# Values, merge gates and branch outputs with tokens as rows, 512 weight channels per matmul

## The chip, the core and the metric

One core of one Trainium2 chip runs the kernel. The metric is the device time of one execution in microseconds (us). In the profile's names PE is TensorE's matmul and PEld its weight load, DVE is VectorE, ACT is ScalarE, POOL is GpSimd and SP issues the DMAs.

## What is computed

Two layers over 256 tokens of 1024 channels, float32. Each layer normalises its input, makes three branches from one wide projection, gates and merges them, projects and adds the residual:

```python
h = rms_norm(x, norm_w)
rq, rk, rv, rg, aq, ak, av, ag, cu, cg, mg = split(h @ w_in + b_in)
r = head_norm(retention(rope(rq), rope(rk), rv)) * ret_norm_w   # 4 heads of 256
y_ret = (r * silu(rg)) @ ret_w_o
a = three dilated attention groups, 8 heads of 128 each, merged by softmax over their sums
y_att = (a * silu(ag)) @ att_w_o
c = silu(layer_norm(causal depthwise conv, 31 taps, of c_lin * sigmoid(c_gate)))
y_conv = (c * silu(cg)) @ conv_w_o
g = sigmoid(mg)                                                  # three gates per channel
x = x + (g[0] * y_ret + g[1] * y_att + g[2] * y_conv) @ w_out
```

After the second layer a last rms_norm gives the output.

## The kernel before, in words

Every weight product is cut into units of 256 channels by 1024 inputs (1 MB), 96 for a layer; `order()` (L60) lists them as (layer, kind, i), and the loop at L802 runs them in that order. The kinds: `cs`, `cl` (convolution gate and input), `rq`, `rk`, `rv`, `rg` (retention), `aq`, `ak`, `av`, `ag` (attention), `cg` (convolution's gate), `mr`, `ma`, `mc` (merge gates), `yr`, `ya`, `yc` (branch outputs), `wo` (output projection).

A unit n goes through four steps. `load` (L171) brings its weights into one of three `raw` tiles, issued three units ahead. `split` (L181), written two units ahead, makes a high part `whi` on ACT (L194, two halves of 1024 columns) and a low part `wlo` on DVE (L195); both have five half-unit buffers, so the second half of unit n + 2 takes the buffer of the first half of unit n. `gemm` (L198) issues 48 products of 128x128 by 256 columns in fp32r: 8 chunks k of the contraction, two halves j, and three products (high x high, high x low, low x high) each. It has three PSUM banks (`g`) in rotation. `finish` (L684) reads the bank.

Most units put channels on the partitions and stream the 256 tokens; only `rv` and `av` put tokens there and stream 256 weight channels. The gates `merge_gate` (L601) are two ACT sigmoids of 256 columns with the bias as a column. `branch` (L607) multiplies product and gate on DVE, adds to `m`, and for `yc` writes `mh` (high on ACT, low on DVE through `hi_lo`, L232), which is the moving operand of `wo`.

Each engine runs what it was given in the order written. In one turn of the loop that is: load(n + 3), split(n + 2), the products of unit n (with the list `inside` in their middle), the list `first`, finish(n), the list `due`, and taps of the convolution, DVE pairs that are handed out by a credit of RATE - COST[kind] per unit, 0.79 for each. Other work is put at a unit by `later` (L717 to 763): scores, softmax and value products of attention, the sums of the convolution's layer norm (`ln_add` at ya 1, `ln_mean` at ya 2, `ln_rows` at ya 3 and mc 2, `ln_rstd` at mc 1).

Of the kernel before, what the change touches and what calls it, by code (L numbers as in the profile page):

```python
# [44 lines left out]
RATE = 2.85  # L45
# [10 lines left out]
COST = {"cs": 0.3, "cl": 1.1, "rq": 1.9, "rk": 1.9, "rv": 2.0, "rg": 1.2, "mr": 0.0, "yr": 0.6,  # L56
        "aq": 2.2, "ak": 2.2, "av": 0.8, "ma": 0.0, "ag": 1.2, "ya": 1.2, "mc": 0.0, "cg": 1.2, "yc": 1.8, "wo": 1.4}


def order():  # L60
    """(layer, kind, i) of every 256-column piece of the weights, in the order of use"""
    u = []
    for l in range(DEPTH):
        def put(kinds, ids):
            u.extend((l, kind, i) for i in ids for kind in kinds)

        def pair(p):
            put(("aq", "ak"), (p, 4 + p, 8 + p))
            put(("av",), (p, 4 + p, 8 + p))
# [11 lines left out]
        put(("ma",), (0,))  # L81
        put(("ag",), four)
        put(("ma",), (1, 2, 3))
        for kind in ("ya", "mc", "cg", "yc", "wo"):
            put((kind,), four)
    return u

# [43 lines left out]
def trunk(ctx: ExitStack, tc, xp, wp, b_in, params, consts, out):  # L131
# [24 lines left out]
    N = len(units)  # L156
    st = {}
# [10 lines left out]
    # ------------------------------------------------------------ weights  # L168
    raw_t, hi_t, lo_t = {}, {}, {}

    def load(n, parts=((0, NK),)):  # L171
        if n >= N:
            return
        t = sb.tile([128, NK, W], F32, tag="raw", name="raw", bufs=3)
        src = wp[n].rearrange("p (k n) -> p k n", n=W)
# [3 lines left out]
        raw_t[n] = t  # L179
# [18 lines left out]
    def gemm(n, a, tokens_first, k_first):  # L198
        """tokens_first: [tokens, channels] out of the product, else [channels, tokens]"""
        hs, ls = hi_t.pop(n), lo_t.pop(n)  # L200
        if n + 1 < N:
# [5 lines left out]
        def part(j, k):  # L207
            wh, wl = hs[k // 4][:, k % 4, :], ls[k // 4][:, k % 4, :]
            t = slice(j * 128, j * 128 + 128)
            if tokens_first:  # L210
                trio = ((a[:, k, 0, t], wh), (a[:, k, 0, t], wl), (a[:, k, 1, t], wh))
            else:
                trio = ((wh[:, t], a[:, k, 0, :]), (wh[:, t], a[:, k, 1, :]), (wl[:, t], a[:, k, 0, :]))
# [17 lines left out]

    def hi_lo(dst, k, v, nk, n=None):  # L232
        """dst: [128, 8, 2, S]; v: fp32 [128, nk, S]"""
# [9 lines left out]
    # ------------------------------------------------------------ norms  # L243
# [3 lines left out]
    def token_sums(tiles, ss=None, more=False):  # L247
        """sums over the partitions of the [128, S] tiles, [tokens, 2]"""
# [35 lines left out]
    def add_squares(key, v, start, stop):  # L284
        """st[key] (+)= v ** 2, two tiles, one of them at the stop"""
# [9 lines left out]
    def unscaled(l, k):  # L295
        """tile k of x * norm_w, before the rstd"""
# [31 lines left out]
    # ------------------------------------------------------------ convolution  # L328
# [77 lines left out]
    # ------------------------------------------------------------ rope  # L406
# [27 lines left out]
    def bias_rows(l, key, c0):  # L434
        bb = sb.tile([128, W], F32, tag="bb", name="bb")
        SP.dma_start(bb, b_in[l:l + 1, c0:c0 + W].to_broadcast([128, W]))
        st[key, "bb"] = bb

    def values(key, p):
        v = sb.tile([128, 2, W], F32, tag="v", name="v")  # L440
        DVE.tensor_tensor(v, p, two(st.pop((key, "bb"))), ALU.add)
        st[key] = v

    def stacked_values(l, pair, g, bb, p):
        """[:, r, c] holds the keys t % 4 == 2 * r + c of both dilated groups: the first of them
        on partitions 64 * c.., the second on the other half."""
        if g == 1:
            st[l, "vs", pair] = sb.tile([128, 2, 2, W], F32, tag="vs", name="vs", bufs=1)
        vs = st[l, "vs", pair]
# [18 lines left out]
    def ret_out(l, h):  # L468
# [9 lines left out]
        rn = sb.tile([128, 2, W], F32, tag="rn", name="rn", bufs=1)  # L478
# [101 lines left out]
    # ------------------------------------------------------------ gates and merge  # L580
# [20 lines left out]
    def merge_gate(l, i, b, p):  # L601
        g = sb.tile([128, 2, S], F32, tag="gt", name="mg", bufs=4)
        for j in range(2):
            ACT.activation(g[:, j], p[:, j], AF.Sigmoid, bias=col(l, P_B + MG // 128 + 8 * b + 2 * i + j))
        st[l, "mg", i] = g

    def branch(l, i, b, n, p):  # L607
        g = st.pop((l, "mg", i))
        if b == 0:
            if i == 0:  # L610
                st[l, "m"] = sb.tile([128, NK, S], F32, tag="m", name="m", bufs=1)
            DVE.tensor_tensor(st[l, "m"][:, 2 * i:2 * i + 2], p, g, ALU.mult)
            return
        m = st[l, "m"][:, 2 * i:2 * i + 2]
        DVE.tensor_tensor(g, p, g, ALU.mult)
        DVE.tensor_tensor(m, m, g, ALU.add)
        if b == 2:
            if i == 0:
                st[l, "mh"] = sb.tile([128, NK, 2, S], F32R, tag="h", name="mh", bufs=1)
            hi_lo(st[l, "mh"], 2 * i, m, 2, n if i < 3 else None)  # L620
# [15 lines left out]
    # ------------------------------------------------------------ end  # L636
# [46 lines left out]
    # ------------------------------------------------------------ program  # L683
    def finish(n, p):  # L684
        l, kind, i = units[n]
# [8 lines left out]
        elif kind in ("rv", "av"):  # L694
            if kind == "av" and i >= 4:
                stacked_values(l, i % 4, i // 4, st.pop((units[n], "bb")), p)
            else:
                values(units[n], p)
        elif kind in ("rg", "ag", "cg"):
            gated(l, i, COLS[kind][1], "c" if kind == "cg" else "ru", n, p)  # L700
        elif kind in ("mr", "ma", "mc"):
            merge_gate(l, i, "rac".index(kind[1]), p)
        elif kind in ("yr", "ya", "yc"):
            branch(l, i, ("r", "a", "c").index(kind[1]), n, p)
        elif l + 1 < DEPTH:
            project(l, i, n, p)
        else:
            project_last(l, i, n, p if n + 1 == N else halves(p))
# [8 lines left out]
    for l in range(DEPTH):  # L717
        for i in range(4):
            b = pos[l, "rq", i]
            later(b + 3, ret_scores, l, i)  # L720
            later(b + 5, ret_out, l, i, at=first)
            later(b + 7, ret_back, l, i, at=first)
# [42 lines left out]
    def warm_up():  # L765
        """keeps the tensor engine busy until the first operands are there, for its clock"""
# [10 lines left out]
    with tc.manual_schedule():  # L777
# [24 lines left out]
        for n, (l, kind, i) in enumerate(units):  # L802
# [6 lines left out]
            if kind in ("rv", "av"):  # L809
# [73 lines left out]
```

## Time and profile before

| | us |
|---|---|
| median of 3 runs | 1215.42 |
| lowest, highest | 1214.85, 1216.55 |
| span of the profiled execution | 1212.8 |
| PE busy | 1202.6 (99% of the span) |
| DVE busy | 994.5 (82%) |
| ACT busy | 742.4 (61%) |
| 16 DMA engines, share of their time | 49% |

The span runs from the first to the last instruction on the core and is 2.6 us under the median of the timed runs; the profiled execution has no time of its own beside it. PE's busy time comes from modelled ends of pipelined matmuls, so how fast it goes is read from the distance of starts and from the length of stretches with a known count, not from the length of one matmul.

### The profile page before, as it was taken

To read this page: it belongs to the slowest core of one execution; us is meant where nothing else is said; L and a number is where in the kernel's file an instruction comes from. 1 tells how busy PE (TensorE), PEld (TensorE's weight loads), DVE (VectorE), ACT (ScalarE), POOL (GpSimd) and SP (SyncE) were. 2 spreads that over 40 slices of the span, in tenths; PEclk is the share of its full clock that TensorE was granted. 3 is DMA by queue.
4 is the path that set the end of the run, shared out by engine and by line. 5 is a ranking of instruction groups with operands and counts; after the bars stand their busy time and mean duration, and the time that the engine had idled before them with its cause. 6 is when DMAs were issued, how large, how long until landed. Compare 5 with 4: busy or idle time off the path is not lost.

```text
span 1212.8 us, 24142 instructions
## 1 busy us (share of the span) xinstructions
PE 1202.6 (99%) x9924; PEld 1195.9 (99%) x9924; DVE 994.5 (82%) x1825; ACT 742.4 (61%) x1140; POOL 9.2 (1%) x17
## 2 busy tenths in 40 slices
PE   9999999999999999999999999999999999999997
PEld 8999999999999999999999999999999999999997
DVE  6988798888888899667789887988898988868674
ACT  6644566759495857366555445587676766664652
POOL 0000000000000000000000000000000000000000
PEclk9999999999999999999999999999999999999999
DMA  8644355445454545555445444544454545455540
GB/s 329 239 161 168 139 202 181 178 148 179 148 179 148 181 160 195 189 181 188 174 161 199 176 148 154 200 178 169 152 178 175 174 154 178 149 209 174 178 170 36
DMA packets 35101, 211.53 MB, mean 174 GB/s; under 512 B 3888, under 2 KB 8752, under 8 KB 10544
## 3 DMA queue, kind: packets, MB, share of 16 engines
q1 hardware_dynamic: 34992, 210.00, 48.8%
q8 instruction: 78, 1.28, 0.4%
q14 instruction: 31, 0.25, 0.1%
HBM read 208.94 MB, written 1.05 MB: 173 GB/s over the span
## 4 chain that ended last, share of the span: by engine, by line
PE 89%; issue 7%; DVE 2%; ACT 1%; DMA 0%; SPq 0%; POOLq 0%; POOL 0%; DVEq 0%; ACTq 0%
PE g L215 82%; PE as L518 2%; PE u L577 1%; PE pt L560 1%; DVE wlo L195 1%; PE rs L459 1%; PE u L573 1%; DMA raw<-in_wp 0%; PE rs L461 0%; PE u L574 0%; PE rt L491 0%; PE r L472 0%; PE r L473 0%; PE r L471 0%; DVE cacc L361 0%
## 5 line engine op out<-in xcount | busy, mean ns | idle before, releaser
L195 DVE TENSOR_TENSOR wlo<-raw,whi 128x1024 fp32r<-128x1024 f32 (+1 forms) x387 | 454.9, 1213 | 76.6 <-ACT whi L194 75.1
L194 ACT CAST whi<-raw 128x1024 fp32r<-128x1024 f32 (+1 forms) x387 | 390.5, 1040 | 135.0 <-PE g L215 127.2
L215 PE MATMUL g<-h,whi 128*128 128x256 f32 x2432 | 439.4, 283 | 0.0
L215 PEld LDWEIGHTS g<-h,whi 128*128 128x128 f32 x2432 | 374.6, 189 | 0.4
L215 PE MATMUL g<-h,wlo 128*128 128x256 f32 x1216 | 343.1, 282 | 0.0
L215 PE MATMUL g<-hp,whi 128*128 128x256 f32 x1280 | 234.0, 285 | 0.0
L215 PEld LDWEIGHTS g<-h,wlo 128*128 128x128 f32 x1216 | 229.3, 189 | 0.0
L361 DVE SCALAR_TENSOR_TENSOR cacc<-cpad,prm,cacc 128x256 f32<-128x256 f32 x480 | 200.9, 480 | 2.2 <-ACT cacc L358 1.9
L215 PEld LDWEIGHTS g<-hp,whi 128*128 128x128 f32 x1280 | 199.9, 192 | 0.4
L215 PE MATMUL g<-hp,wlo 128*128 128x256 f32 x640 | 181.2, 283 | 0.2 <-DVE wlo L195 0.2
L215 PE MATMUL g<-gated,whi 128*128 128x256 f32 x768 | 138.7, 283 | 0.0
L215 PEld LDWEIGHTS g<-hp,wlo 128*128 128x128 f32 x640 | 122.7, 192 | 0.4 <-DVE wlo L195 0.4
L215 PEld LDWEIGHTS g<-gated,whi 128*128 128x128 f32 x768 | 119.7, 192 | 0.0
L215 PE MATMUL g<-gated,wlo 128*128 128x256 f32 x384 | 108.7, 283 | 0.0
L215 PE MATMUL g<-whi,hp 128*128 128x256 f32 x512 | 95.3, 284 | 0.0
L215 PE MATMUL g<-whi,h 128*128 128x256 f32 x512 | 94.7, 283 | 0.0
L215 PEld LDWEIGHTS g<-whi,hp 128*128 128x128 f32 x512 | 80.9, 192 | 0.0
L215 PEld LDWEIGHTS g<-whi,h 128*128 128x128 f32 x512 | 79.7, 188 | 0.0
L215 PEld LDWEIGHTS g<-gated,wlo 128*128 128x128 f32 x384 | 73.7, 192 | 0.0
L215 PE MATMUL g<-gx,whi 128*128 128x256 f32 x384 | 71.7, 289 | 1.8 <-ACT whi L194 1.8
L215 PE MATMUL g<-wlo,hp 128*128 128x256 f32 x256 | 72.4, 283 | 0.0
L215 PE MATMUL g<-wlo,h 128*128 128x256 f32 x256 | 72.0, 281 | 0.0
(144 smaller groups left out, 1399.7 us busy)
## 6 DMA issues: line engine op xcount, KB each, us to landing
raw<-in_wp SPq DMA_DIRECT2D x190, 1024.0 KB, 4.8
bb<-in_b_in SPq DMA_DIRECT2D x32, 128.0 KB, 4.8
cst<-in_consts SPq DMA_DIRECT2D x1, 1344.0 KB, 7.7
raw<-in_wp SPq DMA_DIRECT2D x2, 512.0 KB, 7.6
out_y<-o SPq DMA_DIRECT2D x4, 256.0 KB, 2.4
xt<-in_xp SPq DMA_DIRECT2D x3, 256.0 KB, 5.8
raw<-in_wp SPq DMA_DIRECT2D x3, 256.0 KB, 6.0
cst<-in_consts SPq DMA_DIRECT2D x1, 384.0 KB, 7.6
```

The lines of the kernel that those rows point to most:

```text
L194: ACT.copy(h, t[:, a:b])
L195: DVE.tensor_tensor(lo, t[:, a:b], h.bitcast(F32), ALU.subtract)
L215: PE.matmul(p[j], u, v, start=(k == 0 and i == 0 and (j == 0 or not k_first)), stop=(k == NK - 1 and i == 2 and (j == 1 or not k_first)))
L361: DVE.scalar_tensor_tensor(c[:, 2 * i + j], cp[:, j, t:t + S], col(l, P_TAP + (2 * i + j) * TAPS + t), c[:, 2 * i + j], ALU.mult, ALU.add)
L459: PE.matmul(s[:, 0:256], k[:, d, 0:128], q[:, d, :], start=(d == 0), stop=(d == 1))
L518: PE.matmul(s[:, r], q[:, j, t], k[:, j, t] if g else k[:, j, :], start=True, stop=True)
L560: PE.transpose(p[:, i, r * 128:r * 128 + 128], sm[:, r, o:o + 128], ident)
L573: PE.matmul(u, v[:, 0, d], pts[0][:, 0], start=True, stop=False)
L577: PE.matmul(u[:, t], vs[:, b // 2, b % 2, d], pts[1][:, 0, t], start=False, stop=(b == 3))
```

## The change

The kinds rv, mr, ma, mc, yr, ya, yc, and the two dilated thirds of av, are computed in couples of units with tokens on the partitions: the stationary operand is a 128-token chunk of the activations, and 512 weight channels are streamed at once into a bank. A unit of a couple now holds half of the contraction (four chunks k) of both neighbours, so `load` fetches two halves of two pieces, with rows of 1 KB at the destination. A unit so has 24 products of 512 columns in place of 48 of 256: twelve for the first 128 tokens, then twelve for the second, and a couple takes two banks. What reads the banks (`finish`) runs after the second unit of a couple.

The gates' biases become rows, fetched by DMA, and are added on DVE before the sigmoid. The merged branches `m` have tokens on the partitions, so for `wo` they are turned back by 16 transposes a layer (`merged`). The first two units of `wo` become a couple too (`gemm_two`, products of 256 columns as before), so that the first half of the contraction is done first. `stacked_values` runs once for both dilated groups, retention goes by pairs of heads, two gates of a branch come ahead of `rg` and `ag` in place of one, and RATE and COST are changed. `v` for attention has one buffer instead of two, and `rn` shares one with `pts0`.

```diff
-RATE = 2.85
+RATE = 3.0
-COST = {... "mr": 0.0, "yr": 0.6, ... "av": 0.8, "ma": 0.0, ... "ya": 1.2, "mc": 0.0, ... "yc": 1.8, ...}
+COST = {... "mr": 0.7, "yr": 0.7, ... "av": 1.0, "ma": 0.7, ... "ya": 1.4, "mc": 0.7, ... "yc": 2.1, ...}
+WIDE = ("rv", "mr", "ma", "mc", "yr", "ya", "yc")
@@ order()
-        put(("rq", "rk", "rv"), four)
-        put(("mr",), (0,))
+        for two in ((0, 1), (2, 3)):
+            put(("rq", "rk"), two)
+            put(("rv",), two)
+        put(("mr",), (0, 1))
         put(("rg",), four)
-        put(("mr",), (1, 2, 3))
+        put(("mr",), (2, 3))
...
+def couples(units):
+    c = {}
+    for n, (l, kind, i) in enumerate(units):
+        if kind in WIDE and i % 2 == 0 or kind == "av" and 4 <= i < 8 or kind == "wo" and i == 0:
+            c[n] = c[n + 1] = n
+    return c
@@ load()
+        if n in couple:
+            n0 = couple[n]
+            both = t.rearrange("p (k u) n -> p k u n", u=2)
+            for u in range(2):
+                src = wp[n0 + u].rearrange("p (k n) -> p k n", n=W)
+                SP.dma_start(both[:, :, u, :], src[:, 4 * (n - n0):4 * (n - n0) + 4])
+            yield
+            return
@@ gemm(): tokens_first goes to a function of its own, gemm_values, with the same products
+    def gemm_wide(n, a):
+        hs, ls = hi_t.pop(n), lo_t.pop(n)
+        half = n - couple[n]
+        if half == 0:
+            st["wide"] = [ps.tile([128, 2, W], F32, tag="g", name="g", bufs=3) for _ in range(2)]
+        for t, p in enumerate(st["wide"]):
+            if t == 1:
+                play(inside, n)
+            r = slice(t * 128, t * 128 + 128)
+            for c in range(4):
+                k, d = 4 * half + c, slice(2 * (c % 2), 2 * (c % 2) + 2)
+                wh, wl = hs[c // 2][:, d, :], ls[c // 2][:, d, :]
+                for i, (u, v) in enumerate(((0, wh), (0, wl), (1, wh))):
+                    PE.matmul(p, a[:, k, u, r], v, start=(k == 0 and i == 0), stop=(k == NK - 1 and i == 2))
+        return st["wide"]
+    def gemm_two(n, a):
+        hs, ls = hi_t.pop(n), lo_t.pop(n)
+        half = n - couple[n]
...
+        for u, p in enumerate(st["two"]):
+            if u == 1:
+                play(inside, n)
+            for c in range(4):
+                k, d = 4 * half + c, 2 * (c % 2) + u
+                wh, wl = hs[c // 2][:, d, :], ls[c // 2][:, d, :]
+                for j in range(2):
...
+                    for i, (w, v) in enumerate(trio):
+                        PE.matmul(p[:, j], w, v, start=(k == 0 and i == 0 and j == 0),
+                                  stop=(k == NK - 1 and i == 2 and j == 1))
+        return st["two"]
@@ bias_rows() fetches one or two stretches of 256; ret_values() adds them to both tiles of a couple
-    def stacked_values(l, pair, g, bb, p):
-        for c in range(2):
-            src, o = slice(64 * c, 64 * c + 64), 64 * (c if g == 1 else 1 - c)
-            DVE.tensor_tensor(vs[o:o + 64, :, c, :], p[src], bb[src].unsqueeze(1).to_broadcast([64, 2, W]), ALU.add)
+    def stacked_values(l, pair, ps2):
+        for r in range(2):
+            for c in range(2):
+                src = slice(64 * c, 64 * c + 64)
+                for g in range(2):
+                    o = 64 * (1 - c if g else c)
+                    DVE.tensor_tensor(vs[o:o + 64, r, c, :], ps2[r][src, g], bb[src, g], ALU.add)
@@ merge_gate(), branch()
-        for j in range(2):
-            ACT.activation(g[:, j], p[:, j], AF.Sigmoid, bias=col(l, P_B + MG // 128 + 8 * b + 2 * i + j))
+        for t in range(2):
+            g = sb.tile([128, 2, W], F32, tag="gt", name="mg", bufs=4)
+            DVE.tensor_tensor(g, ps2[t], bb, ALU.add)
+            ACT.activation(g, g, AF.Sigmoid)
+            st[l, "mg", i, t] = g
...
-        m = st[l, "m"][:, 2 * i:2 * i + 2]
-        DVE.tensor_tensor(g, p, g, ALU.mult)
-        DVE.tensor_tensor(m, m, g, ALU.add)
+        for t in range(2):
+            g, m = st.pop((l, "mg", i, t)), st[l, "m"][:, t, i:i + 2]
+            if b == 0:
+                DVE.tensor_tensor(m, ps2[t], g, ALU.mult)
+                continue
+            DVE.tensor_tensor(g, ps2[t], g, ALU.mult)
+            DVE.tensor_tensor(m, m, g, ALU.add)
         if b == 2:
-            hi_lo(st[l, "mh"], 2 * i, m, 2, n if i < 3 else None)
+            for t in range(2):
+                later(n + 1, merged, l, i, t, at=first if i == 0 else inside)
+    def merged(l, i, t):
+        m, mh = st[l, "m"], st[l, "mh"]
+        p = ps.tile([128, 4, 128], F32, tag="pt", name="mt")
+        for j in range(4):
+            PE.transpose(p[:, j], m[:, t, i + j // 2, (j % 2) * 128:(j % 2) * 128 + 128], ident)
+        r = slice(t * 128, t * 128 + 128)
+        hi, lo = (mh[:, 2 * i:2 * i + 4, q, r] for q in range(2))
+        ACT.copy(hi, p)
+        DVE.tensor_tensor(lo, p, hi.bitcast(F32), ALU.subtract)
@@ program
-            later(b + 5, ret_out, l, i, at=first)
-            later(b + 7, ret_back, l, i, at=first)
+            b = pos[l, "rq", i - i % 2]
+            later(b + 3 + 2 * (i % 2), ret_scores, l, i)
+            later(b + 6 + 2 * (i % 2), ret_out, l, i, at=first)
+            later(b + 8 + 2 * (i % 2), ret_back, l, i, at=first)
...
-            finish(n, p)
+            if n not in couple or n > couple[n]:
+                finish(n, p)
```

## Rows read from the trace of the kernel before

**Rows 1.** The page: busy time by engine, and the chain that ended last

```profile
PE 1202.6 (99%) x9924; PEld 1195.9 (99%) x9924; DVE 994.5 (82%) x1825; ACT 742.4 (61%) x1140; POOL 9.2 (1%) x17
PE 89%; issue 7%; DVE 2%; ACT 1%; DMA 0%; SPq 0%; POOLq 0%; POOL 0%; DVEq 0%; ACTq 0%
```

**Rows 2.** The chain in order of time (start us, length us, what): stretches of weight products

```profile
68.90 11.39 PE g L215 x96
466.90 40.37 PE g L215 x336
531.89 80.05 PE g L215 x672
```

**Rows 3.** The same chain: fp32 products of 256 columns, fp32 transposes of 128

```profile
67.60 0.86 PE rs L459 x4
94.35 0.44 PE rt L491 x4
```

**Rows 4.** Timeline of PE (start us, us, line, op, tile): fp32 products of 64 columns

```profile
279.07 1.00 PE L577 MATMUL u<-pts,vs 128*128 128x64 f32 x8
279.91 0.82 PE L560 MATMUL pt<-cst,Sm 128*128 128x128 f32 x6
```

**Rows 5.** PE's timeline at the start, and windows (columns: PE, PEld, DVE, ACT, POOL, PEclk)

```profile
10.32 0.63 PE L215 MATMUL g<-gx,whi 128*128 128x256 f32 x2
10.96 0.63 PE L215 MATMUL g<-gx,whi 128*128 128x256 f32 x2
...
10.50:11.50 1.00, 1.00 (x7) 1.00 (x6) 0.98 (x3) 1.00 (x3) 0.00 (x0) 0.50 1.00 408
...
287.97:347.55 59.58, 59.58 (x494) 59.27 (x493) 51.30 (x112) 41.48 (x73) 0.00 (x0) 1.00 0.48 172
```

**Rows 6.** Groups of instructions by line and shape, DVE and ACT (mean ns of one last)

```profile
L195 DVE TENSOR_TENSOR wlo<-raw,whi 128x1024 fp32r<-128x1024 f32 x382 | 452.0, 1221 | 75.4 <-ACT whi L194 74.0 <-PE g L215 1.1
L452 DVE TENSOR_TENSOR vs<-g,bb 64x512 f32<-64x512 f32 x32 | 22.0, 687 | 0.5
L615 DVE TENSOR_TENSOR mg<-g,mg 128x512 f32<-128x512 f32 x16 | 11.1, 691 | 7.6 <-PE g L215 7.6
L412 DVE TENSOR_TENSOR zz<-z,cst 128x256 f32<-128x256 f32 x16 | 6.8, 425 | 13.7 <-ACT z L411 13.7
...
L194 ACT CAST whi<-raw 128x1024 fp32r<-128x1024 f32 x382 | 387.9, 1047 | 134.0 <-PE g L215 127.2 <-DVE cacc L361 1.8 <-issue 1.6
L562 ACT COPY pts<-pt 128x512 f32<-128x512 f32 x16 | 9.8, 611 | 0.0
```

**Rows 7.** DVE's timeline at the convolution's layer norm, PE's sums (ns, first and last start)

```profile
502.88 0.68 DVE L369 TENSOR_TENSOR ca<-cacc 128x512 f32<-128x512 f32 x1
505.27 2.35 DVE L195 TENSOR_TENSOR wlo<-raw,whi 128x1024 fp32r<-128x1024 f32 x2
522.94 0.42 DVE L259 TENSOR_TENSOR acc<-acc 128x256 f32<-128x256 f32 x1
...
L254 PE MATMUL ss<-cst,ca x4: 168/250/250, 507.1 to 507.4; 128*128 128x1 f32 x4
L254 PE MATMUL ss<-cst,acc x4: 164/250/250, 525.1 to 525.4; 128*128 128x1 f32 x4
```

**Rows 8.** DVE's timeline where the third branch ends and the output projection begins

```profile
583.44 0.69 DVE L615 TENSOR_TENSOR mg<-g,mg 128x512 f32<-128x512 f32 x1 [0.34 <-PE g L215]
```

**Rows 9.** DVE's timeline and PE's chain at the end of an attention pair

```profile
331.09 2.36 DVE L195 TENSOR_TENSOR wlo<-raw,whi 128x1024 fp32r<-128x1024 f32 x2 [0.78 <-ACT whi L194]
...
332.36 5.79 PE g L215 x48
```

**Rows 10.** Windows at 1 KB and 8 KB rows (share, GB/s last), issues by size

```profile
2.50:3.50 1.00, 1.00 (x3) 0.75 (x3) 0.00 (x0) 0.33 (x1) 0.00 (x0) 1.00 0.80 203
...
104.00:106.00 2.00, 2.00 (x19) 2.00 (x18) 1.55 (x4) 1.35 (x3) 0.42 (x1) 1.00 0.90 365
...
raw<-in_wp SPq DMA_DIRECT2D x190, 1024.0 KB, 4.8
```

More of the change, by code (lines that the diff above doesn't have):

```diff
@@ L156, in trunk @@
     N = len(units)
+    couple = couples(units)
     st = {}
@@ L432, in att_rope, with bias_rows, values, ret_values @@
         st[l, what + "a", i] = o
-    def bias_rows(l, key, c0):
-        bb = sb.tile([128, W], F32, tag="bb", name="bb")
-        SP.dma_start(bb, b_in[l:l + 1, c0:c0 + W].to_broadcast([128, W]))
+    def bias_rows(l, key, *c0s):
+        bb = sb.tile([128, 2, W], F32, tag="bb", name="bb")
+        for u, c0 in enumerate(c0s):
+            SP.dma_start(bb[:, u], b_in[l:l + 1, c0:c0 + W].to_broadcast([128, W]))
         st[key, "bb"] = bb
[L439 to L442, printed above, removed]
-    def stacked_values(l, pair, g, bb, p):
-        if g == 1:
-            st[l, "vs", pair] = sb.tile([128, 2, 2, W], F32, tag="vs", name="vs", bufs=1)
-        vs = st[l, "vs", pair]
-        for c in range(2):
-            src, o = slice(64 * c, 64 * c + 64), 64 * (c if g == 1 else 1 - c)
-            DVE.tensor_tensor(vs[o:o + 64, :, c, :], p[src], bb[src].unsqueeze(1).to_broadcast([64, 2, W]), ALU.add)
+    def values(l, i, p):
+        v = sb.tile([128, 2, W], F32, tag="v", name="v", bufs=1)
+        DVE.tensor_tensor(v, p, two(st.pop(((l, "av", i), "bb"))[:, 0]), ALU.add)
+        st[l, "av", i] = v
+    def ret_values(l, i, ps2):
+        v = sb.tile([128, 2, 2, W], F32, tag="v", name="v", bufs=1)
+        bb = st.pop(((l, "rv", i), "bb"))
+        for t in range(2):
+            DVE.tensor_tensor(v[:, t], ps2[t], bb, ALU.add)
+        for u in range(2):
+            st[l, "rv", i + u] = v[:, :, u, :]
+    def stacked_values(l, pair, ps2):
+        vs = st[l, "vs", pair] = sb.tile([128, 2, 2, W], F32, tag="vs", name="vs", bufs=1)
+        bb = st.pop(((l, "av", 4 + pair), "bb"))
+        for r in range(2):
[4 more added lines that the diff above has]
+                    DVE.tensor_tensor(vs[o:o + 64, r, c, :], ps2[r][src, g], bb[src, g], ALU.add)
     def ret_scores(l, h):
@@ new lines, in branch @@
+    def branch(l, i, b, n, ps2):
+        if b == 0 and i == 0:
+            st[l, "m"] = sb.tile([128, 2, NK // 2, W], F32, tag="m", name="m", bufs=1)
+        if b == 2 and i == 0:
+            st[l, "mh"] = sb.tile([128, NK, 2, S], F32R, tag="h", name="mh", bufs=1)
+        for t in range(2):
[5 more added lines that the diff above has]
+            DVE.tensor_tensor(m, m, g, ALU.add)
+        if b == 2:
+            for t in range(2):
+                later(n + 1, merged, l, i, t, at=first if i == 0 else inside)
@@ L684, in finish @@
     def finish(n, p):
-        l, kind, i = units[n]
+        l, kind, i = units[couple.get(n, n)]
         if kind == "cs":
@@ L693, in finish @@
             att_rope(l, i, kind[1], COLS[kind][1], p)
-        elif kind in ("rv", "av"):
-            if kind == "av" and i >= 4:
-                stacked_values(l, i % 4, i // 4, st.pop((units[n], "bb")), p)
+        elif kind == "rv":
+            ret_values(l, i, p)
+        elif kind == "av":
+            if i >= 4:
+                stacked_values(l, i % 4, p)
             else:
-                values(units[n], p)
+                values(l, i, p)
         elif kind in ("rg", "ag", "cg"):
@@ L717, in trunk @@
     for l in range(DEPTH):
-        for i in range(4):
-            b = pos[l, "rq", i]
-            later(b + 3, ret_scores, l, i)
-            later(b + 5, ret_out, l, i, at=first)
-            later(b + 7, ret_back, l, i, at=first)
+        for i in (0, 1, 2, 3):
+            b = pos[l, "rq", i - i % 2]
+            later(b + 3 + 2 * (i % 2), ret_scores, l, i)
+            later(b + 6 + 2 * (i % 2), ret_out, l, i, at=first)
+            later(b + 8 + 2 * (i % 2), ret_back, l, i, at=first)
         for pair in range(4):
@@ L822, in trunk @@
                 src = st[l, "g" if kind in ("cs", "cl") and i < UNSCALED else "h"]
-            p = gemm(n, src, kind in ("rv", "av"), n + 1 < N)
+            if kind == "wo" and n in couple:
+                p = gemm_two(n, src)
+            elif n in couple:
+                p = gemm_wide(n, src)
+            elif kind == "av":
+                p = gemm_values(n, src)
+            else:
+                p = gemm(n, src)
             play(first, n)
```

71 lines of the change are left out of this document (41 added, 30 removed).

## The prediction

> **What bounds the kernel now.** I read the busy sums first: PE is busy for 1202.6 of 1212.8 us, DVE for 994.5 [rows 1]. The chain that ended last lies on PE for 89%, and the 7% called issue is its last stretch, where the view has lost the releasers; PE is busy there too. So the kernel takes as long as PE's instruction stream, plus small waits. How fast is that stream? In the chain in order of time, divide the length of a stretch by its count: 118.6 ns for a product of 256 columns in the retention stage (11.39 us for 96), 120.1 around ag, ma and ya (40.37 for 336), 119.1 from mc to wo (80.05 for 672) [rows 2]. The granted clock is full (1.00 in the window of [rows 5]), at which 256 columns stream in 106.7 ns. Some 12 ns of each product are thus not streaming, and the question is whether they are paid per product or per column.
>
> Three rows bear on it. An fp32 product is in the records as two instructions, which stream two cycles per column; 256 columns take 0.86 / 4 = 215 ns, for 512 cycles of 213.3 [rows 3]. A longer stream under one weight load so has almost nothing on top. The same form with 64 columns, 53 ns of stream, still takes (279.91 - 279.07) / 8 = 105 ns [rows 4]: something that doesn't shrink with the columns, most likely the weight load. And where the clock was at the lower level (0.50, 1.2 GHz), three fp32r products of 256 columns took 10.96 - 10.32 = 0.64 us, 213 each: exactly the stream, nothing on top [rows 5]. All three fit one reading: a product takes the longer of its stream and a floor of the weight path, just under 119 ns here.
>
> **The wide products.** 56 units outside attention and 16 av units (36 a layer) turn 48 products of 256 into 24 of 512. The trace shows no fp32r product of 512; the nearest row is the 512-cycle fp32 instruction, 215 ns, and I take that. The bounds are 213.3, the bare stream, and 239, two of the present ones. With 8 units at 118.6, 16 at 120.1 and 32 at 119.1 the mean is 119.3, so a wide product saves 238.6 - 215 = 23.6 ns: 56 x 24 x 23.6 = 31.7 us, and 16 x 24 x 23.6 = 9.1 us in av. A wide unit takes 24 x 0.215 = 5.16 us instead of 5.73.
>
> The Trainium skill (TensorE: Matmul & The Clock Gate, Back-to-back issue gap) gives the isolated distance at full clock as columns / 2.4 plus 2.5 ns. By that rule two products of 256 take 218.4 ns and one of 512 takes 215.8, and the change would save 2.6 ns each, an estimated 4.5 us in all. The trace disagrees for 256 columns (118.6 to 120.1 where the rule says 109.2, [rows 2]); no run here shows 512.
>
> **The transposes.** 16 a layer, 32 in all, on PE's path: four existing ones take 0.44 us [rows 3], so 32 x 0.11 = 3.5 us.
>
> **What waits behind a couple.** Two things move the work on DVE later. The first half of a unit's weight buffers is free only at 75% of a wide unit (both token chunks pass over it), against 50% before. ACT's cast (1.05) and DVE's low part (1.22) [rows 6] that were waiting for it come after, and `finish` stands behind that low part on DVE's queue: with T for the end of a couple on PE, the low part ends at T - 1.29 + 1.05 + 1.22 and hand-offs, T + 1.1. Before, `finish` began 0.2 to 0.3 after the unit (583.44 for a unit that ended about 583.2, [rows 8]). And `finish` of a branch is four operations of 0.69 [rows 6] at once. So they end at T + 3.9.
>
> *Layer norm of the convolution.* `ln_add` follows the second ya on DVE and took 505.27 - 502.88 = 2.4; PE's sums came at 507.1, with 1.8 to spare [rows 7]. In the changed order it ends at T + 3.9 + 2.4 = 6.3, and PE, which has only one wide unit between, is there at T + 5.2: 1.1 us of wait. The second sum has the same form: from the end U of ya, DVE has 1.1, eleven operations of 0.69, two low parts of 1.22, the fold of 0.42 and one gap behind an ACT square (0.6 to 0.7, as the 128x512 pass of 0.61 in [rows 6]), together 12.3; PE is there after ln_rows (0.45) and two units, U + 10.8: 1.5. Before, the fold ended at 523.36 and PE came at 525.1 [rows 7]. A layer loses 2.6, both 5.2 us.
>
> *From yc to wo.* The transposes of the last couple stand in the middle of the first wo unit. PE gets there at T + 2.9, the first four go through to 3.3, the other four need DVE's fourth operation at 3.9: 0.6. Then 24 products end at 7.2. ACT's two copies of the turned tiles (0.61 each) stand behind a cast that waits for the twelfth of these products (5.8): cast to 6.9, copies to 8.1. DVE's low part goes to 8.1, its two subtractions to 9.5. The next wo unit wants both at 7.2: 0.9 for the high part, 1.3 more for the low. 2.8 a layer, 5.6 us. Before, three operations and a cast fitted under the 4.3 us until the last two chunks were wanted.
>
> *Attention pairs.* At the end of a pair DVE's low part of the unit after next starts at 331.09, its first half ends 1.2 later, and PE begins that unit at 332.36 [rows 9]: no cover is left. The chain there runs from stacked values over the reciprocal, ACT's multiplications, a cast, to that low part. Two wide av units bring PE there 1.1 us sooner; the chain isn't shorter, since four additions of 0.69 become eight of 64x256, 0.34 (half of 0.687) to 0.42 [rows 6], though four of them leave the place ahead of the softmax. What PE gains, it waits: 8 x 1.1 = 9.1 us given back. DVE is busy for 51.3 of 59.6 us of a pair [rows 5], so the wait doesn't grow from pair to pair.
>
> *Merge gates.* 24 additions of 0.69 come onto DVE. In the six wide units from mr to yr a couple has two splits (4.9), two operations (1.4) and, at RATE 3.0 less 0.7, 4.6 us of taps: 10.9 against PE's 10.3. Three couples run over by 1.8 a layer, and PE's next bank is wanted 2.58 after a couple while its reader ends at 1.1 + 0.7: cover of 0.8. I take 0.5 a layer, 1.0 us; bounds 0 and 3.6.
>
> **At nothing.** The loads get rows of 1 KB. In a window of such rows 203 GB/s went at a share of 0.80, 254 at full share; at 8 KB 365 at 0.90, 406 [rows 10]. 1 MB so takes 4.1 us of a unit's 5.16, and the landing, 4.8 us now, grows by 1.5; a raw tile is free almost two units (some 9 us) before its cast. Without that cover each late microsecond would be one of PE, 76 times. SP issues two DMAs per such unit instead of one, and 24 more fetches of bias rows in all (56 in place of 32); it mostly waits for buffers. ACT's sigmoids become half as many, of double width. Retention by pairs has rows of slack: its values are wanted a whole unit later. The wo couple's products keep their size.
>
> **The sum.** 1212.8 - 31.7 - 9.1 + 3.5 + 5.2 + 5.6 + 9.1 + 1.0 = 1196.4 for the span. The median of the runs lies 2.6 above the span: 1199.0. About 0.2% (2.4 us) is what a measurement of this kernel can tell from no change.
>
> **The rivals.**
> (A) *No floor of the weight path: the 12 ns go with the columns,* that is, an fp32r stream runs at 2.15 columns per ns and 512 take 239. Nothing is saved, the transposes (3.5) and the wo wait (5.6) stay, the layer norm waits shrink by the 1.1 us of two slower units to about 1, attention loses nothing: 1215.4 + 10.1, about 1226. This is slower than before. The saving has to reach some 12 ns a product, 227 instead of 239, before the change pays. For it: no fp32r row with another width at full clock; the slow-clock row fits it too. Against: 105 ns at 64 columns. The rule of the Trainium skill above would end near here, at about 1221. Chance 0.14.
> (B) *The 12 ns are a fixed addition to any product,* 225 for 512: half the saving, 1728 x 13.3 = 23 us, with waits in between (transposes 3.5, wo 5.6, layer norm 3.6, attention 5, gates 0.5): about 1211. Against it: 215 for 512 cycles [rows 3]. Chance 0.14, of which half faster, a third the same.
> (C) *The waits don't appear,* because DVE and ACT overlap more than I lay end to end: 1215.4 - 40.8 + 3.5 plus half of the waits in wo, 1181 to 1190. For it: ACT waited 127 us for PE in its casts [rows 6], so there is room in general. Chance 0.11.
> (D) *DVE becomes the bound in the attention pairs and in mr to yr,* with the tap rate raised: one more tap pair in each chain and twice my waits there, 10 to 14 us on top: 1209 to 1213, at worst 1217. Against: 51.3 of 59.6 us. Chance 0.06.
>
> **How the numbers follow.** My own case, 1192 to 1208, has 0.55. Faster: 0.55 + 0.11 + 0.07 from B + 0.02 from D; same: 0.05 from B and 0.03 from D; slower: 0.14 from A, 0.02 from B, 0.01 from D. Rounded, 0.74, 0.08, 0.18. The range from 1185 to 1222 leaves out the better part of A above and a third of C below, with the tails of the rest under 0.2.
>
> **What would show it.** After: stretches of wide products with 215 to 216 ns from start to start; PE waiting for DVE at the sums of the layer norm, at the second half of the turned tiles and at the second wo unit; wide av units shorter, but a pair only as long as now, about 59.5 us. Distances of 225 or 239 refute the first step. A pair of 58.4 or less refutes the attention term.

## The result and the profile after

The changed kernel takes 1235.14 us (median; 1232.94 to 1235.83) beside 1215.34 for the kernel before: a ratio of 1.0159, 95% interval 1.0144 to 1.0173. It is 1.6% slower; the forecast was 1199.0, and 1235 lies outside the range of 1185 to 1222. The profiled execution has a span of 1233.3 us.

The page of the kernel after, busy time by engine and shares of the chain that ended last, the lines that answer to [rows 1]:

```profile
PE 1201.0 (97%) x8228; PEld 1116.6 (91%) x8228; DVE 1012.0 (82%) x1881; ACT 739.0 (60%) x1116; POOL 9.2 (1%) x17
PE 65%; DVE 19%; issue 9%; ACT 5%; DMA 0%; SPq 0%; POOL 0%; DVEq 0%; POOLq 0%; ACTq 0%
```

PE is now idle for 1233.3 - 1201.0 = 32.3 us, before for 10.2, and DVE and ACT carry 24% of the chain where they had 3%. PE's idle time by what ended it, kernel after (us in total, times, longest):

```profile
PE g L283 <- DVE vs L538: 7.8, 2, 4.3
PE g L237 <- DVE vs L538: 5.7, 6, 1.4
PE g L283 <- DVE mg L692: 2.7, 2, 1.5
PE g L302 <- DVE mh L721: 2.2, 2, 1.1
PE ss L328 <- DVE ca L333: 1.4, 2, 0.7
...
PE g L302 <- ACT mh L720: 1.1, 2, 0.6
PE ss L328 <- DVE acc L333: 1.0, 2, 0.5
```

L283 is a product of 512 columns, L237 one of 256, L302 one of the `wo` couple; L538 adds the bias to the stacked values, L692 to the gates, L720 and L721 write the turned tiles' high and low parts. The chain in order of time, kernel after (start, length, what; compare [rows 2]):

```profile
69.11 11.16 PE g L283 x48
...
483.54 20.77 PE g L283 x90
...
565.48 16.38 PE g L283 x72
581.86 0.87 PE mt L717 x8
...
597.52 7.36 PE g L302 x47
604.89 17.14 PE g L237 x144
```

A product of 512 columns takes 11.16 / 48 = 232.5 ns on `h` (rv), 16.38 / 72 = 227.5 on the gated branches (yc), and 20.77 / 90 = 230.8 where ma and ya follow each other. The forecast had 215, against 238.6 for the two products it replaces.

To see where the time is lost, cut both timelines of PE at the same marks: the first score product of each attention pair, the first product of ya, the first of `wo`, and the start of the next layer (in layer 2 the last sum of squares).

| stage, us | layer 1 before | after | layer 2 before | after |
|---|---|---|---|---|
| start to the first pair | 228.3 | 227.9 | 219.1 | 218.8 |
| three pairs | 179.1 | 180.0 | 178.6 | 180.7 |
| last pair, ma, ag, to ya | 82.4 | 86.7 | 82.6 | 87.5 |
| ya, mc, cg, yc, to wo | 93.4 | 93.4 | 93.4 | 93.4 |
| wo, to the end | 22.8 | 28.1 | 24.5 | 28.3 |

The change gains 0.7 us ahead of the first pairs and loses 21.3: 9.2 between the last pair and ya, 9.1 from wo on, 3.0 in the other pairs. Two places carry the loss.

**The last pair.** Three timelines of the kernel after (start, length, line, what). ACT, then DVE, then PE:

```profile
440.10 0.60 ACT L626 ACTIVATE Sm<-Sm,nm 128x384 f32<-128x384 f32 x1
440.61 0.18 ACT L626 ACTIVATION_READ_ACCUMULATOR Sm<-Sm,nm 128x1 f32 x1
440.70 1.98 ACT L218 CAST whi<-raw 128x1024 fp32r<-128x1024 f32 x2
```

```profile
441.77 2.36 DVE L219 TENSOR_TENSOR wlo<-raw,whi 128x1024 fp32r<-128x1024 f32 x2 [0.89 <-ACT whi L218]
444.16 3.49 DVE L538 TENSOR_TENSOR vs<-g,bb 64x256 f32<-64x256 f32 x8
```

```profile
439.58 0.40 PE L283 MATMUL g<-whi,h 128*128 128x512 f32 x1
...
442.15 0.40 PE L283 MATMUL g<-whi,h 128*128 128x512 f32 x1
446.04 0.47 PE L283 MATMUL g<-whi,h 128*128 128x512 f32 x1 [3.49 <-DVE vs L538]
...
448.46 1.06 PE L283 MATMUL g<-whi,h 128*128 128x512 f32 x2
449.31 0.63 PE L283 MATMUL g<-wlo,h 128*128 128x512 f32 x1
449.74 1.06 PE L283 MATMUL g<-whi,h 128*128 128x512 f32 x2
```

Here a couple (ma 0, 1) follows a couple (av) directly. There are three banks: ma's first 128 tokens take the third, from 439.58, and the next 128 need the bank of the couple before. Its readers are the first four of the eight additions (until about 445.9). They start at 444.16, 4.6 us after the end of the couple, behind a low part that waited for a cast, which stood behind the pair's exponentials. In an ordinary pair a unit of 256 columns is next and has a free bank for all of its 5.7 us; there the wait is 1.4 at most. And a second loss stands behind the first: windows of the kernel after (the clock of PE is the column after POOL):

```profile
448.00:450.00 2.00, 2.00 (x6) 1.60 (x5) 1.48 (x4) 2.00 (x5) 0.00 (x0) 0.50 0.15 61
...
598.00:606.00 8.00, 8.00 (x58) 8.00 (x58) 2.14 (x3) 2.11 (x2) 0.00 (x0) 0.82 0.28 117
```

After the wait of 3.49 us the granted clock is 0.50 (1.2 GHz), and a product takes (449.74 - 448.46) / 3 = 427 ns. That is 512 columns at 1.2 GHz, with nothing on top.

**From yc to wo.** PE's timeline, kernel after:

```profile
590.90 0.60 PE L717 MATMUL mt<-cst,m 128*128 128x128 f32 x4
591.98 0.63 PE L717 MATMUL mt<-cst,m 128*128 128x128 f32 x4 [0.48 <-DVE m L707]
...
596.03 0.38 PE L302 MATMUL g<-mh,whi 128*128 128x256 f32 x1 [0.55 <-ACT mh L720]
597.52 0.58 PE L302 MATMUL g<-mh,whi 128*128 128x256 f32 x1 [1.11 <-DVE mh L721]
```

The three waits stand where the forecast put them, at 0.48, 0.55 and 1.11 (0.6, 0.9 and 1.3 forecast). What it didn't have is what follows in layer 1: the clock falls to the lower level behind them (0.82 as the mean of the 8 us after), and the 47 products from 597.52 take 7.36 us, 157 ns each; at 119 they take 5.6. But the fall doesn't always follow. In layer 2 of the same execution the waits are the same, 0.48, 0.55 and 1.11, and the clock stays at 1.00:

```profile
1206.06 0.39 PE L302 MATMUL g<-mh,whi 128*128 128x256 f32 x1 [1.11 <-DVE mh L721]
...
1190.00:1215.00 25.00, 22.86 (x166) 21.21 (x165) 15.65 (x22) 8.89 (x12) 0.00 (x0) 1.00 0.12 44
```

So the stage from wo on loses 5.3 us in layer 1 and 3.8 in layer 2.

### The profile page after: what moved, and what is told of

Read it like the earlier page. It is cut to its first block, busy times and chain, and to the rows that moved or that the text cites. A ratio compares the mean times of both kernels' runs of the same rounds, so it can differ in the third digit from the quotient of the medians.

```text
span 1233.3 us, 20935 instructions
## 1 busy us (share of the span) xinstructions
PE 1201.0 (97%) x8228; PEld 1116.6 (91%) x8228; DVE 1012.0 (82%) x1881; ACT 739.0 (60%) x1116; POOL 9.2 (1%) x17
## 4 chain that ended last, share of the span: by engine, by line
PE 65%; DVE 19%; issue 9%; ACT 5%; DMA 0%; SPq 0%; POOL 0%; DVEq 0%; POOLq 0%; ACTq 0%
PE g L237 41%; PE g L283 17%; DVE wlo L219 8%; DVE cacc L435 3%; DVE Sm L608 2%; ACT whi L218 2%; ACT Sm L626 1%; PE as L604 1%; DVE vs L538 1%; PE u L663 1%; PE pt L646 1%; PE g L302 1%; DVE m L707 1%; PE rs L545 1%; PE u L659 1%
## 5 line engine op out<-in xcount | busy, mean ns | idle before, releaser
L237 PE MATMUL g<-h,whi 128*128 128x256 f32 x1664 | 301.5, 284 | 5.7 <-DVE vs L538 5.7
L237 PEld LDWEIGHTS g<-h,whi 128*128 128x128 f32 x1664 | 257.4, 189 | 7.6 <-issue 6.8
L237 PE MATMUL g<-h,wlo 128*128 128x256 f32 x832 | 235.4, 283 | 0.0
L237 PE MATMUL g<-hp,whi 128*128 128x256 f32 x1280 | 233.9, 285 | 0.0
L237 PEld LDWEIGHTS g<-hp,whi 128*128 128x128 f32 x1280 | 200.2, 192 | 0.9
L237 PE MATMUL g<-hp,wlo 128*128 128x256 f32 x640 | 181.0, 283 | 0.0
L283 PE MATMUL g<-whi,h 128*128 128x512 f32 x512 | 168.5, 403 | 7.8 <-DVE vs L538 7.8
L237 PEld LDWEIGHTS g<-h,wlo 128*128 128x128 f32 x832 | 156.8, 188 | 0.0
L283 PEld LDWEIGHTS g<-whi,h 128*128 128x128 f32 x512 | 97.9, 191 | 30.9 <-issue 8.6
L283 PE MATMUL g<-whi,gated 128*128 128x512 f32 x384 | 120.9, 391 | 2.7 <-DVE mg L692 2.7
L237 PEld LDWEIGHTS g<-hp,wlo 128*128 128x128 f32 x640 | 122.6, 192 | 0.0
L283 PE MATMUL g<-wlo,h 128*128 128x512 f32 x256 | 102.2, 399 | 0.0
L283 PEld LDWEIGHTS g<-whi,gated 128*128 128x128 f32 x384 | 72.1, 188 | 18.5 <-DVE mg L692 3.6
L283 PE MATMUL g<-whi,hp 128*128 128x512 f32 x256 | 82.3, 393 | 0.0
L283 PE MATMUL g<-wlo,gated 128*128 128x512 f32 x192 | 74.8, 390 | 0.0
L237 PE MATMUL g<-gx,whi 128*128 128x256 f32 x384 | 72.6, 291 | 1.2 <-ACT whi L218 1.2
L237 PEld LDWEIGHTS g<-gx,whi 128*128 128x128 f32 x384 | 61.9, 198 | 1.7 <-ACT whi L218 1.5
L502 DVE TENSOR_TENSOR zz<-zz,cst 128x512 f32<-128x512 f32 x48 | 33.2, 692 | 31.7 <-ACT zz L501 30.6
```

The source lines that it names most:

```text
L237: PE.matmul(p[j], u, v, start=(k == 0 and i == 0 and (j == 0 or not k_first)), stop=(k == NK - 1 and i == 2 and (j == 1 or not k_first)))
L283: PE.matmul(p, a[:, k, u, r], v, start=(k == 0 and i == 0), stop=(k == NK - 1 and i == 2))
L502: DVE.tensor_tensor(zz, zz, two(cst[:, sin:sin + S]), ALU.mult)
```

## The experiments

All ratios are to the kernel before, timed on the same chip. Diffs are against the changed kernel unless another is named.

**The price of a product by itself.** This kernel leaves the computation out and was run once. It has only products, with an fp32r stationary tile that changes for each: 512, 384, 256 and 128 columns, then 512 and 256 beside ACT and DVE at work, 512 beside DMA, and 512 with one stationary tile for twelve products.

```diff
+for columns, count in ((512, 48), (384, 64), (256, 96), (128, 96)):
+    p = bank()
+    for n in range(count):
+        PE.matmul(p[:, :columns], stat(n), w[:, n % 4, :columns], start=(n == 0), stop=(n == count - 1))
```

> Leaves the whole computation out: rows of fp32r products alone, each with a new stationary operand, in blocks of 512, 384, 256 and 128 columns; then 512 and 256 beside casts on ACT and subtractions on DVE, 512 beside four loads of 1 MB, and 512 with the stationary operand changed only every twelfth product. If a product pays a fixed addition (theory), the blocks show 213 + 12 = 225 to 232 ns at 512, 160 + 12 = 172 at 384, 119 at 256, 65 or more at 128. If only a floor of the weight path counts (the forecast), 215, 162, 119, 110 to 119. If the addition goes with the columns (rival A), 239, 179, 119, 60. If the 227 to 232 of the changed kernel come from the other engines' traffic, the quiet block shows 215 and the blocks beside ACT and DVE, or beside the loads, more.

Its chain in order of time:

```profile
28.33 10.88 PE g L175 x48
39.21 11.12 PE g L178 x64
50.33 11.51 PE g L181 x96
61.83 10.67 PE g L184 x96
...
78.04 10.88 PE g L197 x48
88.92 11.51 PE g L200 x96
...
105.90 10.88 PE g L210 x48
116.78 10.88 PE g L214 x48
```

The last block (L214) in a window, with the products (x46), the weight loads (x46) and the granted clock:

```profile
116.80:127.00 10.20, 10.20 (x46) 8.45 (x46) 0.00 (x0) 0.02 (x1) 0.00 (x0) 1.00 0.72 239
```

226.7 ns for 512 columns, 173.8 for 384, 119.9 for 256, 111.1 for 128. Less the streams at 2.4 GHz (213.3, 160.0, 106.7) that is 13.4, 13.8 and 13.2 on top: the same at every width from 256 to 512. Only at 128 columns does something else take over. The other engines, the DMA and a stationary tile that stays the same (L197, L210, L214) change nothing. In that last block the tile was loaded anew for each product all the same (46 loads beside 46 products), so it doesn't show whether the addition belongs to the load. Rival B's forecast of the price holds at full clock; a wide product saves 2 x 119.9 - 226.7 = 13.1 ns.

**A unit between the last couple of av and ma.** One ag unit goes first, so that no couple follows a couple there.

```diff
-        put(("ma",), (0, 1))
-        put(("ag",), four)
+        put(("ag",), (0,))
+        put(("ma",), (0, 1))
+        put(("ag",), (1, 2, 3))
```

> The changed kernel with one unit of ag moved between the last av couple and the first couple of ma in each layer, so that the couple's second bank is wanted a unit later. Theory: in the changed kernel PE waits 3.5 to 4.3 us there for the stacked values to be read, and loses about 1 us more at the lower clock behind it, in each layer; without it 1226, give or take 2. If it is DVE's amount of work that delays (rival), the wait moves on to the next couples and the time stays at 1235.

1226.1 us, 1.0101 (1.0085 to 1.0118), 9.0 less. The waits of that couple, second line below (line numbers are one higher), fall from 7.8 to 1.9, while the others stay as they were, and the clock is 1.00 in the window from 446 to 470 us (last line), where it was 0.93. So the wait comes from the bank, and with it goes the low clock that was behind it.

```profile
PE g L238 <- DVE vs L539: 5.7, 6, 1.4
...
PE g L284 <- DVE vs L539: 1.9, 2, 1.3
...
446.00:470.00 24.00, 23.84 (x152) 21.42 (x153) 21.56 (x39) 18.98 (x27) 0.00 (x0) 1.00 0.54 184
```

The low clock has moved elsewhere in this run. The waits behind yc are as in the changed kernel (0.48, 0.57 and 1.1), but now the clock stays up in layer 1 and falls in layer 2:

```profile
1196.60:1199.80 3.20, 3.20 (x17) 3.20 (x16) 0.25 (x1) 0.00 (x0) 0.00 (x0) 0.50 0.00 0
```

By the marks of the table above, the stage from wo on takes 26.6 us in layer 1 without the fall and 28.1 with it (changed kernel), in layer 2 28.3 without (changed kernel) and 29.8 with it: a fall costs 1.5 us.

**The turned tiles ahead of the weights' cast.** The parts of the third `wo` unit's weights are written behind the turned tiles.

```diff
-            late = n < 3 or (kind, i) == ("cs", 0)
+            late = n < 3 or (kind, i) in (("cs", 0), ("wo", 0))
```

> The changed kernel with the casts of the third wo unit written behind the turned tiles' copies instead of ahead of them. Theory: PE's two waits at the second wo unit (0.6 and 1.1 us) and the lower clock behind them (about 1.8 us) go, in both layers: 1228, give or take 2; the wait for DVE's fourth operation (0.5) stays. If the wait there is for DVE's branch work (rival), 1234 to 1236.

1229.67 us, 1.0123 (1.0107 to 1.0138), 5.5 less. The two waits at L302 are gone, and its chain has the couple's second unit and the first's end at 118.6 ns a product:

```profile
591.94 8.54 PE g L302 x72
```

By stages, from wo on, 3.7 us go in layer 1 and 2.2 in layer 2. The 2.2 are mostly the two waits, which from start to start of the products cost 2.1 (0.55 and 1.11 of it are listed as idle); the 1.5 more in layer 1 is the fall of the clock, which layer 2 never had. The wait behind av is still there in this run, and in layer 1 no fall follows it:

```profile
447.07 0.48 PE L283 MATMUL g<-whi,h 128*128 128x512 f32 x1 [3.48 <-DVE vs L538]
...
447.00:452.00 5.00, 4.93 (x21) 4.07 (x22) 3.44 (x10) 3.03 (x6) 0.00 (x0) 1.00 0.44 184
```

There the stage from the last pair to ya takes 85.0 us, where the changed kernel takes 86.7.

**Both.** The two edits together.

> The two edits at once: a unit of ag ahead of the first ma couple, and the casts of the third wo unit behind the turned tiles. Theory: the two waits lie in different stages and add up, 9.0 + 5.4: 1220.7, give or take 1.5. If a common resource is behind both (rival), less than the sum: 1224 or more.

1220.42 us, 1.0045 (1.0028 to 1.0062). 1235.1 - 9.0 - 5.5 = 1220.6: they add up.

**The values alone, and the gates and branches alone.** In the first only `rv` and the dilated `av` are couples, in the second only gates, branches and the first `wo` units.

```diff
-WIDE = ("rv", "mr", "ma", "mc", "yr", "ya", "yc")
+WIDE = ("rv",)
...
```

(gates, branches, wo, RATE and COST but for av go back to the kernel before)

> Only values wide: rv and the dilated av; gates, branches and wo as in the kernel before, RATE and COST as before but for av. Theory: 24 units save 24 x 6 to 12 ns each, 5 to 6 us, and the attention pairs give it back in waits for the stacked values: 1213 to 1218. If the pairs' DVE work is what makes the changed kernel slower (rival), 1223 or more.

```diff
-WIDE = ("rv", "mr", "ma", "mc", "yr", "ya", "yc")
+WIDE = ("mr", "ma", "mc", "yr", "ya", "yc")
-        if kind in WIDE and i % 2 == 0 or kind == "av" and 4 <= i < 8 or kind == "wo" and i == 0:
+        if kind in WIDE and i % 2 == 0 or kind == "wo" and i == 0:
...
```

(rv, av, their order and their additions go back to the kernel before)

> Only gates and branch outputs wide, with the transposes and the wo couple; rv, av, their order and their additions as in the kernel before. RATE and the COST of the gates and branches as in the changed kernel. Theory: attention pairs as short as before (59.5 us), nothing between the last pair and ya; the products save 10 us, transposes (3.5), wo (about 9 with the lower clock), layer norm sums (2.4 to 3.4) and the gates from mr to yr (2.7) cost 18: 1222, give or take 3. If the gates' additions on DVE are the main loss (rival), the pairs are longer too and the time is 1230 or more.

Values alone: 1221.25 us, 1.0054 (1.0039 to 1.0069), slower by 6.6 where 1213 to 1218 was expected and the rival had 1223 or more, so it fits neither; PE waits 9.5 us for the stacked values, eight times, once a pair, and behind the longest of these the clock falls once. Gates and branches alone: 1222.89, 1.0065 (1.0050 to 1.0080), the time as expected, though its wo stages lost 7.6 us and not 9, with no fall of the clock in either. The two add to 14.7 us of loss, the whole change has 19.8. The missing 5.1 can be put to the wait after the last pair, which needs av and ma as couples both: with the values alone the longest wait for stacked values is 2.6, in the whole change 4.3. That is an argument; the run that puts a unit between is what shows the wait's price.

**The tap rate and the costs of before.** The taps are handed out as in the kernel before.

```diff
-RATE = 3.0
+RATE = 2.85
-COST = {... "mr": 0.7, "yr": 0.7, ... "av": 1.0, "ma": 0.7, ... "ya": 1.4, "mc": 0.7, ... "yc": 2.1, ...}
+COST = {... "mr": 0.0, "yr": 0.6, ... "av": 0.8, "ma": 0.0, ... "ya": 1.2, "mc": 0.0, ... "yc": 1.8, ...}
```

> The changed kernel with RATE and the whole COST table of the kernel before, so taps are handed out as before. Theory: the waits are for banks and for the order of queues; tap placement moves them little: 1233 to 1237. If the raised tap rate overloads DVE in the pairs (rival D), 1225 to 1229.

1235.73 us, 1.0171 (1.0156 to 1.0186): no effect. That part of rival D falls.

**What is left with the losses taken out.** `av` narrow as before, the third `wo` unit's parts late, and the layer norm's steps moved: the first sum a unit earlier, the second half a unit later.

```diff
-        if kind in WIDE and i % 2 == 0 or kind == "av" and 4 <= i < 8 or kind == "wo" and i == 0:
+        if kind in WIDE and i % 2 == 0 or kind == "wo" and i == 0:
-            late = n < 3 or (kind, i) == ("cs", 0)
+            late = n < 3 or (kind, i) in (("cs", 0), ("wo", 0))
-        later(y + 1, ln_add, l)
+        later(y, ln_add, l)
-        later(c + 1, ln_rstd, l)
+        later(c + 2, ln_rstd, l)
...
```

> The changed kernel with the dilated av in single units as before (rv stays wide), the wo casts behind the turned tiles, ln_add a unit earlier and the second half of the layer norm a unit later. Theory: the waits between av and ma (9.3 by stages), in the pairs (3.4), half of wo (5.4) and the layer norm's (2.4) go: 1213 to 1216, level with the kernel before; better than 1211 only if wide gates and branches are worth more than the 10 us of their shorter products less transposes and the waits from mr to yr. If the loss is DVE's total load (rival), 1222 or more.

1213.85 us, 0.9993 (0.9984 to 1.0003): level with before. Its largest waits:

```profile
PE g L283 <- DVE mg L689: 3.8, 4, 1.5
...
PE mt L714 <- DVE m L704: 1.0, 2, 0.5
```

**Gates apart from branches.** Against the kernel just told of:

```diff
-        put(("mr",), (0, 1))
-        put(("rg",), four)
-        put(("mr",), (2, 3))
+        for two in ((0, 1), (2, 3)):
+            put(("mr",), two)
+            put(("rg",), two)
...
```

(the same for ma and ag)

> The kernel of the run e7_best, with one more change: two of the four rg (and ag) units now stand between the first and the second couple of merge gates, and the other two behind the second, so that no couple of branches follows a couple of gates directly. Theory, a couple whose first bank is still being read waits for it: the four waits of the products for the gates' bias additions (3.8 us in all, the longest 1.5) go, and up to 1 us comes back elsewhere, since DVE is full there: 1210.5 to 1211.5, under the kernel before by 0.3%. Rival, DVE's load and not the bank sets the time in this stage: the waits move to the low parts of the weights and the time stays 1213 to 1214.5.

1214.45 us, 0.9998 (0.9989 to 1.0007). The rival is right on the time, though the wait went to another place than it said: the gates' waits fall from 3.8 to 1.1, but the second couple of yr now waits 2.6 us for the products with m, ahead of which DVE still has its queue:

```profile
PE g L283 <- DVE m L701: 2.6, 2, 1.3
```

**The activations' tiles elsewhere in SBUF.** Against the last one; h and the gated tile lie ahead of the weight buffers, which move up.

```diff
+    for tag, shape in (("gated", [128, NK, 2, S]), ("h", [128, NK, 2, S])):
+        sb.tile(shape, F32R, tag=tag, name=tag, bufs=1)
     with tc.manual_schedule():
```

> The kernel of e9_order, with the tiles of the activations (h, and the one that the gated branches use) placed at low addresses of SBUF, 43232 and 59616 bytes into a partition, ahead of the weight buffers; in all kernels so far h lies at 164960, the gated tile at 112864. Theory, the 5 us-thousandths between a wide product on h (232 ns) and one on the gated tile (227 ns) come from where h lies: all wide products take 226 to 228 ns, and 32 wide units of 24 products win 5 ns each, 3.8 us, so about 1207. Rival, they come from what else runs on the core in those stages: the distances stay 232 and 227, and the time is that of e9_order.

1214.28 us, 0.9996 (0.9987 to 1.0005). Its chain:

```profile
69.19 10.92 PE g L283 x48
...
88.47 11.51 PE g L237 x96
...
558.67 16.35 PE g L283 x72
```

The theory is right on the distances: the rv products go from 11.16 to 10.92 us for 48, 227.5 ns, as those of yc (16.35 / 72 = 227.1). It is wrong on the time. Nearly all products of 256 columns now take 119.8 to 120.2, where the kernel before had many at 118.5 to 119.3, and the waits for gates and for m grow by 0.9. By the mean distances of the two runs, the products of 256 columns on h and on the merged branches took some 2.7 us more in all, so together this is about what the wide products won. Which tile's place it is (h or the weights that stream) isn't told apart, since both moved.

**A unit between the couples of yr.** Against the last one:

```diff
-        put(("yr",), four)
-        put(("cs", "cl"), (3,))
+        put(("yr",), (0, 1))
+        put(("cs",), (3,))
+        put(("yr",), (2, 3))
+        put(("cl",), (3,))
-            later(pos[l, "cs", 3], by_residue, l, part, 4)
+            later(pos[l, "cl", 3], by_residue, l, part, 4)
```

> The kernel of e10_place, with one unit of the convolution (cs 3) moved between the two couples of yr, so that these don't follow each other either. Theory, bank waits of a couple behind a couple: the two waits for the products with m (2.8 us in all, 1.5 the longest) go, and the time is 1211.0 to 1212.0, under the kernel before by 0.2% to 0.3%. Rival, DVE is full from mr to yr (between 180 and 200 us it has no idle time), so what PE doesn't wait there it waits behind, at the weights' low parts: 1213.5 to 1214.5.

1214.28 us, 0.9996 (0.9987 to 1.0005). The waits for m are gone, and one of the same size is there at the start of attention, for the permuted copy of h that ACT can only write once yr is through, with one unit fewer behind yr to cover it:

```profile
PE g L239 <- ACT hp L589: 2.6, 2, 1.3
PE g L285 <- DVE mg L691: 1.8, 2, 0.9
```

No version here is faster than the kernel before by more than a measurement tells.

## Why the prediction was wrong, point by point

**The step that failed first: "a product takes the longer of its stream and a floor of the weight path".** From the three rows that it called on ([rows 3], [rows 4], and the slow clock of [rows 5]) it read a floor of 119 ns, but two were fp32 instructions and the third ran at the lower clock; none was an fp32r product of another width at full clock, which it said itself. At full clock an fp32r product has 13 to 14 ns on top at 256, 384 and 512 columns alike. At the lower clock there is nothing on top at either width (213 ns at 256, [rows 5], 427 at 512), so that row could not tell a floor from an addition. In the kernel a wide product saves less still: 238.6 - 232.5 = 6.1 ns on h, 238.6 - 227.5 = 11.1 on the gated branches, and 13 in av, 240 - 226.7. The last is from two starts in PE's timeline, kernel after, with 18 products between them (4.08 us):

```profile
428.22 0.62 PE L283 MATMUL g<-whi,hp 128*128 128x512 f32 x2
...
432.30 0.62 PE L283 MATMUL g<-whi,hp 128*128 128x512 f32 x2
```

With 32 units on h and 24 on the branches, 24 products each, that is 4.7 + 6.4 = 11.1 us in place of 31.7: a term too large by 20.6. In av it is 5.0 in place of 9.1.

**The wait that it didn't have: a couple behind a couple.** The working gave T + 1.1 for when the reading of a couple begins, and asked in each place which unit comes next, except after the last pair. There are three banks and a couple holds two, so the second half of the next couple waits for the first one's readers. It took this into account for the gates ("cover of 0.8") and not for ma behind av, where the readers begin at T + 4.6 behind the exponentials. Price: 9.0 us, clock included, by the run that puts a unit between.

**The clock behind a wait.** No term had it. In the profiled execution the clock fell to 1.2 GHz behind both long waits at ma and behind the waits of wo in layer 1, and a fall costs about 1.5 us (1.7 by layer 1's two times between the last pair and ya): some 4.5 of the 20 us lost. It doesn't follow from the wait alone: behind the same waits the clock stayed up in layer 2, and at ma in layer 1 of the run with the late cast. What decides it stays open.

**The terms that held.** Eight transposes of `mt` took 0.87 us, 0.11 each. The layer norm waits were put in the right two places, at 1.1 and 1.5, and are 0.7 and 0.5: 2.4 us in all instead of 5.2. The three waits of wo are there, 2.1 for 2.8 in either layer; beyond its eight transposes (0.87) the stage lost 4.4 in layer 1, where the clock fell, and 2.9 in layer 2. DMA didn't matter, as it said: no wait for a load is in the list. The attention pairs gave the gain of av back, as it said, but not just that: 59.7, 60.5 and 59.7 us in the first layer for 59.5, 59.6 and 60.0, and 3.0 us over both layers that it didn't have. The gates' waits for a bank were taken at 1.0 and are 2.7.

**The sum again, with measured terms.** 1199.0 + 20.6 (wide products outside attention) + 3.0 (pairs) + 10.4 (after the last pair: 9.2 and the 1.2 that ma gained there) + 1.8 (wo, 9.1 for 5.6 and two times 0.87) - 2.8 (layer norm) + 1.7 (gates) = 1233.7, beside 1235.1. The falls of the clock are in the stages' losses here, so the sum holds for an execution with three of them.

**The rivals.** B had the price of the product right, 225 ns forecast and 226.7 measured, but its time, 1211, has the same two gaps. A's time, 1226, came nearest, by luck and for a wrong reason: the addition doesn't grow with the columns. D was wrong on the tap rate, and right that DVE would set the pace from mr to yr: with the waits at one couple taken away, the next one has them. C falls.

The Trainium skill (TensorE: Matmul & The Clock Gate, Back-to-back issue gap) gives 215.8 ns for an isolated product of 512 columns at full clock; the trace disagrees, 226.7 measured in a stream of such products alone and 227 to 232 in the kernel. By its rule two of 256 and one of 512 differ by 2.5 ns, measured are 13.1.

## What to carry to other kernels

A price that the trace doesn't show for the very form and type is the first thing to measure: it decided 20 us here, and rows of another type at the same width pointed the wrong way. When an operation takes two buffers of three at once, go through every place where two such operations meet, and ask when the readers of the first begin, with all that stands ahead of them on their engine. A fall of the clock that one profile shows behind a wait is looked for behind the same wait in the other layer and in other runs, before it is priced into the kernel. Where an engine is full behind a bound one, the time that one wins is waited for at the next hand-over: the version without the two great waits saves some 11 us of products, pays 3.5 for its transposes and 4.8 in the two waits shown, the rest in places that aren't told apart here, and is level.

## What the runs showed of the hardware

At full clock an fp32r product has a fixed addition of 13 to 14 ns from 256 to 512 columns, whether other engines or DMA are at work beside it or not, and costs 111 ns at 128 columns; at 1.2 GHz it takes 213 and 427 ns at 256 and 512 columns, the bare stream. The place of the tiles in SBUF changes the distance of products by some 2%: 232.5 or 227.5 ns at 512 columns, 118.5 or 120 at 256; by what rule stays open. PE's granted clock fell to 1.2 GHz in the middle of a kernel, behind one wait of 3.5 us, and also behind three waits of 0.48, 0.55 and 1.11 us; behind the same waits in the other layer, or in another run, it stayed at 1.00.
